# A streaming encoder step: the mixer's input projection in half-sized products, x kept in DRAM, and one pool for the mixer and the first feed-forward stage

## The chip, the cores and the metric

The kernel runs on one core of a Trainium2 chip. The metric is the time of one execution on the device in microseconds (us): the median over several runs, beside one execution that the hardware profiler recorded and from which the profile is made.

## The reference

Two layers over 1024 prompt frames and 32 frames of a running stream, of 1024 features each, in float32. Layer 0 is what matters here:

```python
def _mixer_a(h, ctx, w_in, conv_w, w_out):
    gb, gc, u = jnp.split(h @ w_in, 3, axis=-1)
    z, new_ctx = _causal_dwconv(gc * u, ctx, conv_w)      # three taps along time
    return (gb * z) @ w_out, new_ctx

def _conv_ffn(h, ctx, w_up, conv_w, w_down):
    up = h @ w_up
    upc, new_ctx = _causal_dwconv(up, ctx, conv_w)
    g, v = jnp.split(upc, 2, axis=-1)
    return (jax.nn.silu(g) * v) @ w_down, new_ctx

# layer 0
x = x + _mixer_a(_rmsnorm(x, a_norm), ...)        # w_in: 1024 x 3072, w_out: 1024 x 1024
x = x + _conv_ffn(_rmsnorm(x, ffn_norm), ...)     # w_up: 1024 x 5632, w_down: 2816 x 1024
# layer 1: attention over keys and values of x, then a second _conv_ffn; last a norm
```

## The kernel before, in words

Features lie on the 128 partitions, the 1056 frames (1024 + 32) in the free dimension, so x is 8 tiles of 128 x 1056. Each float32 product is made of three reduced-precision ones: both operands are split into a high part (a copy by ScalarE, ACT) and a low part (a subtraction by VectorE, DVE), and TensorE (PE) adds high x high, high x low and low x high (`chain`, L253, for whole products; `product`, L882, for half-sized ones). A weight of 128 output features is called a unit: 8 blocks of 128 x 128.

**Mixer, plain products.** `opening` (L712) loads x and the first three units (gc, u and gb of tile 0), splits x times the norm's gain into 16 resident tiles `xs`, and runs 3 x 72 matmuls of 352 columns: 8 blocks, 3 parts, 3 column pieces `CH`. Beside them it sums the squares of x for the norm, and near its end PE makes three products of a diagonal with ones (the "broadcasts") that spread the frames' scale `rstd` over the partitions; DVE then multiplies the results by it. `mixer` (L832) runs `make` for each of the 8 feature tiles: three units of 72 matmuls of 352 columns (`unit`, L275), u x gc, the convolution (`conv`, L520: ACT the first tap, DVE two), times gb, split into a high and a low act. After four tiles, `down` adds the first half of the output projection to x in SBUF, in pieces of 352 columns (L559 to L567). The second half goes through `tokenwise` (L435): four pieces of 264 frames (`ENDS`), after each of which the next norm of those frames is made, and x is written to DRAM (`xd`). `resident` (L504) holds its four units.

**Feed-forward, half-sized products.** `begin` (L590) and `plain` (L939) make the first four units with blocks of x split into quadrants (feature half 1 or 2, frame half 1 or 2; `part`, L480: b11, b12, b21, b22). Then DVE forms sums and differences of quadrants, again split (t1 to t4), and every `pair` (L892) makes two units by seven products of half size where a plain 2 x 2 x 2 blocking has eight: weight sums on GpSimd (POOL), 7 weight splits (`operand`, L874), 7 x 24 matmuls of 264 columns, and adds from PSUM on ACT and DVE (`late`, L959, the last frames in three pieces). Down products of two acts at a time (`stream`, L1063) are dealt out between a pair's steps; PE's result goes by ACT to a tile `xs`, and a DMA of POOL's queue adds it to x in DRAM. At the end `load` (L162) brings x back.

**What sets the order.** Each engine works through its own queue in order, and so do the DMA queues of SP and POOL. In `strict` parts the order is the program's; elsewhere a scheduler sets it. A tile comes from a rotating pool and waits until the last reader of its buffer is done: `keep` (24 of 128 x 1056 for x and its splits), `slot` (20 in the mixer, 14 in the feed-forward stages), weights `w` (4), one raw weight `wraw`. PSUM is 3 + 2 x 2 + 1 banks in the mixer, 2 + 3 x 2 in the feed-forward stages (`UPBANKS`). The mixer and the first feed-forward stage are two phases with pools of their own (L1587 to L1600).

Of the kernel before, what the change touches and what calls it, by code (L numbers as in the profile page):

```python
# [26 lines left out]
TT = SEQ + DEC  # L27
# [17 lines left out]
SLOTS = 20  # L45
# [41 lines left out]
class Net:  # L87
# [134 lines left out]
    def weights(self, src, gain=None, keep=False, cuts=((0, 8),), raw=None):  # L222
        nc = self.nc
        raw = raw or self.wp.tile([128, NK, 128], F32, name="wraw", bufs=1)
# [8 lines left out]
        h, l = (self.keep(n, [128, NK, 128], F32R) if keep else self.wp.tile([128, NK, 128], F32R, name=n, tag="w")  # L233
# [19 lines left out]
    def chain(self, ps, w, xs, c, ks=None):  # L253
# [3 lines left out]
        for i in ks or range(n):  # L257
            (xh, xl), (wh, wl) = xs[i], w[i]
            nc.tensor.matmul(ps, wh, xh[:, c[0]:c[1]], start=(i == 0), stop=False)  # L259
            nc.tensor.matmul(ps, wh, xl[:, c[0]:c[1]], start=False, stop=False)  # L260
            nc.tensor.matmul(ps, wl, xh[:, c[0]:c[1]], start=False, stop=(i == n - 1))  # L261
# [173 lines left out]
    def tokenwise(self, weight, acts, x, scale, units):  # L435
# [14 lines left out]
        for c in ENDS:  # L450
            cs, n = slice(*c), c[1] - c[0]
            if c is ENDS[-1]:
# [85 lines left out]
    def down_steps(self, units, acts, x, done=None, lag=False):  # L538
# [3 lines left out]
        banks = self.singles() if lag else iter(self.dbank, None)  # L542
# [47 lines left out]
    def begin(self, x, early, late):  # L590

# [3 lines left out]
        us = [self.slot("u", [128, WID]) for _ in range(2)]  # L595
        one, two = (slice(*c) for c in HALVES)
        orders = tuple(range(NK)), LATER
# [18 lines left out]
        def second(k):  # L616
            q = x[k + k2]
            self.nc.vector.tensor_sub(q[:, two], q[:, two], x[k][:, one])
            self.nc.vector.tensor_sub(q[:, one], q[:, two], q[:, one])

        for i in range(2):
# [30 lines left out]
        sums = [(n, k, x[k + d][:, h]) for n, ks, d, h in (  # L652
            ("t1", range(k2), 0, one), ("t3", (2, 3), 0, two), ("t2", range(k2), k2, two), ("t3", (0, 1), 0, two),
            ("t4", range(k2), k2, one)) for k in ks]
        for k in range(k2):
            self.job(lambda k=k: first(k), 1.4)
        for k in range(k2):
            self.job(lambda k=k: second(k), 1.4)
        todo = [made(*t) for t in sums]
        for (high, _), (_, low) in zip(todo + [(None, None)], [(None, None)] + todo):  # L660
            if high:
                self.job(high, 0)
            if low:
                self.job(low, 0.7)
# [47 lines left out]
    def opening(self, x, gain):  # L712
# [35 lines left out]
        def evict(u, i):  # L748
            for p, d in spread(CH[i], before[u]):
# [11 lines left out]
        before = (0, PAD, 0)  # L761
        out = [self.slot("gc"), self.slot("u", [128, TC + PAD]), self.slot("gb")]
        banks = [[self.dbank()[:, :c[1] - c[0]] for c in CH] for _ in range(2)]
# [20 lines left out]
        sq = [self.slot("sq") for _ in range(NK)]  # L784
        for m in range(NK):
            ACT.activation(sq[m], x[m], AF.Square)
            if m:
                DVE.tensor_add(sq[0], sq[0], sq[m])
# [7 lines left out]
        banks.append([self.dbank()[:, :c[1] - c[0]] for c in CH])  # L796
# [4 lines left out]
        ps = self.bank("s")[:SIDE, :n]  # L801
        for i in range(n):
            PE.matmul(ps[:, i:i + 1], sq[0][:, i * SIDE:(i + 1) * SIDE], self.ones[:, :1], start=True, stop=True)
# [10 lines left out]
        self.chain(banks[2][1], ws, xs, CH[1])  # L814
        for i, c in enumerate(CH):
# [4 lines left out]
            ps = self.bank("sos"[i])[:, :c[1] - c[0]]  # L820
            PE.matmul(ps, self.ones[:SIDE], dg[:, b].rearrange("p n c -> p (n c)"), start=True, stop=True)
            ACT.activation(self.rs[:, slice(*c)], ps, AF.Copy)
        for i, c in enumerate(CH):
            if i == 2:
                self.chain(banks[2][i], ws, xs, c)
            for u in range(2):
                for p, d in spread(c, before[u]):
                    DVE.tensor_mul(out[u][:, d], out[u][:, d], self.rs[:, p])
            DVE.tensor_mul(out[2][:, slice(*c)], banks[2][i], self.rs[:, slice(*c)])
        return xs, out  # L830

    def mixer(self, x, xs, opened, after):  # L832
        a, nc = self.a, self.nc
# [869 lines left out]
```

## Time and profile before

| | us |
|---|---|
| median of 3 runs (2506.28 to 2509.9) | 2508.73 |
| the profiled execution | 2509.51 |
| its span, first to last instruction | 2507.7 |
| PE busy | 2460.4 (98%) |
| DVE busy | 1521.1 (61%) |
| ACT busy | 1216.9 (49%) |
| POOL busy | 890.3 (36%) |
| PE's granted clock, mean | 0.995 |

Matmuls are pipelined, so one's duration is longer than the distance from one to the next; the distance is read from the number of matmuls in a stretch in which PE never waits. Instructions of `strict` parts carry the line of a helper (L73 before, L72 after), others their own. A wait is put down to the instruction that released it last.

### The profile page before, as it was taken

How to read it: one execution, taken by the hardware profiler on the slowest of the kernel's cores; microseconds unless marked ns; L12 is line 12 of the kernel's file. 1: busy time of each engine (PE TensorE's matmuls, PEld its weight loads, DVE VectorE, ACT ScalarE, POOL GpSimd, SP SyncE). 2: the span in 40 equal slices, each digit the busy share in tenths (PEclk: the TensorE clock that was granted, in tenths of full speed). 3: DMA queues.
4: the chain of work that ended last, by engine and by line, in shares of the span. 5: the costliest groups of instructions: out<-in, count | busy, mean ns of one | idle time of the engine just before them, and what ended most of it. 6: DMA issues, size and time to landing. Idle time of an engine off the chain costs nothing. (4 is left out here: it accounts for less than half of the span.)

```text
span 2507.7 us, 47246 instructions
## 1 busy us (share of the span) xinstructions
PE 2460.4 (98%) x18484; PEld 2424.6 (97%) x18484; DVE 1521.1 (61%) x2622; ACT 1216.9 (49%) x2394; POOL 890.3 (36%) x969
## 2 busy tenths in 40 slices
PE   8999999999999999999999999999999999999997
PEld 8999999999999999998999999999999999999997
DVE  6434448755555555666677667665874555555566
ACT  4111124645555555445666666643554555555554
POOL 0000012444443344452544445412244444433442
PEclk9999999999999999999999999999999999999998
DMA  3111222476666666532322233373247766666662
GB/s 121 46 48 43 60 88 82 88 121 118 121 119 113 120 112 121 134 114 66 83 71 77 75 80 81 78 250 100 70 93 124 119 119 116 114 117 120 120 153 70
DMA packets 145583, 254.76 MB, mean 102 GB/s; under 512 B 22352, under 2 KB 58320, under 8 KB 145360
## 3 DMA queue, kind: packets, MB, share of 16 engines
q0 software_dynamic: 44032, 86.53, 24.3%
q1 hardware_dynamic: 101328, 165.21, 22.1%
q8 instruction: 145, 2.38, 0.4%
q14 instruction: 78, 0.64, 0.1%
HBM read 130.52 MB, written 113.04 MB: 97 GB/s over the span
## 5 line engine op out<-in xcount | busy, mean ns | idle before, releaser
L889 PE MATMUL pb_p<-b,wb 128*128 128x264 f32 x6720 | 895.2, 285 | 1.9 <-ACT u L931 1.9
L889 PEld LDWEIGHTS pb_p<-b,wb 128*128 128x128 f32 x6720 | 850.3, 188 | 2.3 <-ACT u L931 2.3
L1078 POOL DMA_DIRECT2D xd<-xs x288 | 261.9, 914 | 495.0 <-ACT xs L1076 486.7
L1076 ACT ACTIVATE xs<-pb_d 128x264 f32<-128x264 f32 x576 | 218.4, 387 | 349.2 <-PE pb_d L261 310.3
L259 PE MATMUL pb_d<-acth,wb 128*128 128x264 f32 x1152 | 327.9, 285 | 1.5 <-ACT xs L1076 1.5
L260 PE MATMUL pb_d<-actl,wb 128*128 128x264 f32 x1152 | 327.4, 284 | 0.0
L261 PE MATMUL pb_d<-acth,wb 128*128 128x264 f32 x1152 | 327.2, 285 | 0.0
L259 PE MATMUL pb_d<-xh,wh 128*128 128x384 f32 (+2 forms) x816 | 269.1, 330 | 0.9 <-DVE x L564 0.7
L261 PE MATMUL pb_d<-xh,wl 128*128 128x384 f32 (+2 forms) x816 | 266.4, 326 | 0.0
L260 PE MATMUL pb_d<-xl,wh 128*128 128x384 f32 (+2 forms) x816 | 266.2, 326 | 0.0
L532 DVE SCALAR_TENSOR_TENSOR y<-u,cv,y 128x1058 f32<-128x1058 f32 x178 | 228.8, 1329 | 52.1 <-ACT y L528 52.0
L259 PEld LDWEIGHTS pb_d<-acth,wb 128*128 128x128 f32 x1152 | 216.7, 188 | 2.4 <-ACT xs L1076 2.1
L260 PEld LDWEIGHTS pb_d<-actl,wb 128*128 128x128 f32 x1152 | 216.9, 188 | 0.0
L261 PEld LDWEIGHTS pb_d<-acth,wb 128*128 128x128 f32 x1152 | 216.9, 188 | 0.0
L514 POOL COPY u<-cv 128x4 f32<-128x4 f32 x96 | 65.1, 678 | 374.5 <-DVE u L845 274.5
L236 ACT ACTIVATE wh<-wraw 128x1024 fp32r<-128x1024 f32 x63 | 66.8, 1061 | 247.9 <-PE pb_o L260 114.9
L879 DVE TENSOR_TENSOR wb<-wr,wb 128x512 fp32r<-128x512 f32 x196 | 153.0, 782 | 54.8 <-ACT wb L878 44.5
L879 DVE TENSOR_TENSOR wb<-ws,wb 128x512 fp32r<-128x512 f32 x160 | 121.2, 759 | 98.8 <-ACT wb L878 98.8
L911 POOL TENSOR_TENSOR ws<-wr 128x512 f32<-128x512 f32 x80 | 123.4, 1543 | 135.4 <-DMA wr<-in_w_up 108.3
L259 PEld LDWEIGHTS pb_d<-xh,wh 128*128 128x128 f32 x816 | 154.1, 189 | 1.8 <-issue 1.0
L878 ACT ACTIVATE wb<-wr 128x512 fp32r<-128x512 f32 x196 | 123.4, 629 | 66.4 <-PE pb_p L889 58.2
L260 PEld LDWEIGHTS pb_d<-xl,wh 128*128 128x128 f32 x816 | 154.3, 189 | 0.3
(383 smaller groups left out, 5063.6 us busy)
## 6 DMA issues: line engine op xcount, KB each, us to landing
xd<-xs POOLq DMA_DIRECT2D x288, 264.0 KB, 4.3
wr<-in_w_up SPq DMA_DIRECT2D x168, 256.0 KB
wr<-in_w_down SPq DMA_DIRECT2D x80, 256.0 KB
wraw<-in_w_in SPq DMA_DIRECT2D x21, 512.0 KB
xd<-x SPq DMA_DIRECT2D x64, 132.0 KB
x<-xd POOLq DMA_DIRECT2D x32, 264.0 KB, 5.3
wraw<-in_w_kq SPq DMA_DIRECT2D x16, 512.0 KB
xd<-x SPq DMA_DIRECT2D x16, 264.0 KB
```

What stands on the lines that cost most here:

```text
L236: nc.scalar.activation(h[:, i:j], raw[:, i:j], AF.Copy)
L259: nc.tensor.matmul(ps, wh, xh[:, c[0]:c[1]], start=(i == 0), stop=False)
L260: nc.tensor.matmul(ps, wh, xl[:, c[0]:c[1]], start=False, stop=False)
L261: nc.tensor.matmul(ps, wl, xh[:, c[0]:c[1]], start=False, stop=(i == n - 1))
L514: self.nc.gpsimd.tensor_copy(v, st.rearrange("p (a b) -> p a b", b=2))
L532: self.nc.vector.scalar_tensor_tensor(y, u[:, i:i + TC], w[:, i:i + 1], y, op0=OP.mult, op1=OP.add)
L878: nc.scalar.activation(t[:, 0], src, AF.Copy)
L879: nc.vector.tensor_sub(t[:, 1], src, t[:, 0].bitcast(F32))
L889: nc.tensor.matmul(ps[:, q, :QB], w[:, i, k], t[:, j, cs], start=(begin and k == 0 and n == 0), stop=(end and k == len(b) - 1 and n == 2), ...
L911: getattr(self.nc.gpsimd, "tensor_" + op)(dst, x, y)
L1076: nc.scalar.activation(t[:, q * QB:(q + 1) * QB], ps, AF.Copy)
L1078: nc.gpsimd.dma_start(d, t, accum_op=OP.add)
```

## The change

The mixer now runs in the feed-forward's pool (14 slots, `UPBANKS`), in one phase with the first feed-forward stage.

- `opening` gets its third gate's last chain ahead of the broadcasts, and loads one unit more.
- Tile 1's three units are made by plain products of 352 columns, from the `xs` tiles. Meanwhile DVE norms the 8 tiles of x in place, and as PE lets `xs` tiles go, ACT and DVE split x into quadrants (`part`) and form the sums t1 to t4 (`sums`, taken out of `begin`).
- gc and u of tile 2 go through `plain`: half-sized blocks, no product saved.
- The other 16 units are 8 pairs: (gc, u) of tiles 3 to 7, and gb of tiles 2 and 3, 4 and 5, 6 and 7. What follows of a unit (u x gc, taps, gate, split) is dealt out two steps behind each product (`put_off`).
- x as loaded is spilled to DRAM at the start. The first four acts of the output projection go through `stream` in twos, which adds to it there, in pieces of 264 columns; then x is loaded back by POOL's queue, and `tokenwise` does the last four acts, with the first two acts' products of six tiles ahead (`ahead=2`).

```diff
     def tokenwise(self, weight, acts, x, scale, units, ahead=0):
...
+            early = [next(banks)[:, :n] for _ in range(6)] if ahead and c is ENDS[0] else []
+            for m, ps in enumerate(early):
+                self.chain(ps, weight(m), acts, c, range(ahead))
             for m in range(NK):
-                ps = next(banks)[:, :n]
-                self.chain(ps, weight(m), acts, c)
+                ps = early[m] if m < len(early) else next(banks)[:, :n]
+                self.chain(ps, weight(m), acts, c, range(ahead, g) if m < len(early) else None)
...
     def opening(self, x, gain, after):
...
+        h, l = self.weights(a["w_in"][after])
...
         self.chain(banks[2][1], ws, xs, CH[1])
+        self.chain(banks[2][2], ws, xs, CH[2])
         for i, c in enumerate(CH):
...
         for i, c in enumerate(CH):
-            if i == 2:
-                self.chain(banks[2][i], ws, xs, c)
...
+    def mixer(self, x, after):
+        with self.strict():
+            xs, opened, w = self.opening(x, 0, NK + 1)
+        for m in range(NK):
+            self.spill(x, m)
...
+        with self.strict():
+            two = [weight(2 * NK + 1)]
+            for i, c in enumerate(CH):
+                self.chain(banks[0][i], w, xs, c)
+                if i:
+                    scaled(0, i - 1)
+                if i < 2:
+                    for m in LATER[2 * i:2 * i + 2]:
+                        norm(m)
+            two.append(weight(1, self.slot))
+            scaled(0, 2)
+            for m in LATER[4:]:
+                norm(m)
...
+            for n in range(NK + 1):
+                for u, k in ((0, LATER[n:n + 1]), (1, LATER[n - 1:n] if n else ())):
+                    for t, c in zip(banks[u + 1], CH):
+                        self.chain(t, two[u], xs, c, k)
+                if n:
+                    parts(LATER[n - 1])
+                if n in (3, 5):
+                    sums[n // 2 - 1]()
+                    sums[n // 2 + 3]()
...
+        put_off = gate(0, opened[2]) + parts[0] + gate(1, one[2]) + parts[1]
+        for i, (t, gates) in enumerate(((3, 0), (2, 1), (4, 0), (5, 0), (4, 1), (6, 0), (7, 0), (6, 1))):
+            if i in (1, 3):
+                for _ in fill:
+                    pass
+                fill, n, at, span = self.stream(a["w_out"][i - 1:i + 1], acts[i - 1:i + 1]), many, 0, 7 * (i // 2 + 2)
+            steps = self.pair(a["w_in"][top], a["w_in"][low], b, us)
+            for todo in steps if i else [steps[j] for j in (0, 2, 1, 3, 4, 5, 6)]:
+                for f in todo + tuple(put_off[:2]):
+                    f()
...
+        for m in range(NK):
+            self.load(x, m, nc.gpsimd)
+        ws = self.resident(a["w_out"][4:], True)
+        with self.strict():
+            self.tokenwise(ws, acts[4:], x, after, self.first(0), 2)
...
-    with net.phase(SLOTS):
+    with net.phase(UPSLOTS, banks=UPBANKS):
         net.fresh = 0
-        with net.strict():
-            opened = net.opening(x, 0)
-        net.mixer(x, *opened, net.normalise(x, 1))
-    with net.phase(UPSLOTS, banks=UPBANKS):
+        net.mixer(x, net.normalise(x, 1))
...
-        "w_out": down_units(i["w_a_out"][0]),
+        "w_out": down_units(i["w_a_out"][0], (2, 2, 4)),
```

Three places show how the queues change. The first is PE's queue at the end of the opening: `pb_...` are PSUM tiles, `xh`, `xl`, `wh`, `wl` the high and low parts of x and a weight, `dg,ones` the broadcasts. Before:

```order
L73 MATMUL pb_d<-xh,wl 128x352
L73 MATMUL pb_s<-dg,ones 128x352
L73 MATMUL pb_o<-dg,ones 128x352
L73 MATMUL pb_s<-dg,ones 128x352
L73 MATMUL pb_d<-xh,wh 128x352
```

Now, at the same place:

```order
L72 MATMUL pb_p<-xh,wh 128x352
L72 MATMUL pb_p<-xl,wh 128x352
L72 MATMUL pb_p<-xh,wl 128x352
L72 MATMUL pb_d<-dg,ones 128x352 x3
L72 MATMUL pb_p<-xh,wh 128x352
```

The last chain of 24 matmuls moved from behind the broadcasts to ahead of them; what follows them now is the next unit.

The second is DVE's queue, where it multiplies the opened units by `rstd`. `gc`, `u`, `gb` are units, `y` the convolved one, `actl` an act's low part. Before:

```order
L73 TENSOR_TENSOR gc<-gc,rstd 128x352
L73 TENSOR_TENSOR u<-u,rstd 128x320
L73 TENSOR_TENSOR u<-u,rstd 128x32
L845 TENSOR_TENSOR u<-u,gc 128x1024
L845 TENSOR_TENSOR u<-u,gc 128x32
L73 TENSOR_TENSOR gb<-pb_d,rstd 128x352
L532 SCALAR_TENSOR_TENSOR y<-u,cv,y 128x1058 x2
L853 TENSOR_TENSOR y<-y,gb 128x1024
```

Now, with `x_99` to `x_106` the eight tiles of x, `wl` a weight's low part and `wraw` the weight as loaded:

```order
L72 TENSOR_TENSOR gb<-pb_p,rstd 128x320
L72 TENSOR_TENSOR gb<-pb_p,rstd 128x32
L72 TENSOR_TENSOR wl<-wraw,wh 128x1024
L72 SCALAR_TENSOR_TENSOR x_99<-x_99,gain,rstd 128x1056
L72 SCALAR_TENSOR_TENSOR x_103<-x_103,gain,rstd 128x1056
L864 TENSOR_TENSOR u<-u,gc 128x1024
L864 TENSOR_TENSOR u<-u,gc 128x32
L72 TENSOR_TENSOR u<-pb_p,rstd 128x352
L72 SCALAR_TENSOR_TENSOR x_100<-x_100,gain,rstd 128x1056
L72 SCALAR_TENSOR_TENSOR x_104<-x_104,gain,rstd 128x1056
L72 TENSOR_TENSOR u<-pb_p,rstd 128x352
```

The convolution of tile 0 moved far back; a weight's low part and the norms of x stand in its place, with the next unit's scalings between them.

The third is the DMA queue of SP. Before, weights of the input projection follow the loads of the opening:

```order
L724 DMA x_106<-in_x 128x1056
L727 DMA wr<-in_w_in 128x1024
L708 DMA cv<-in_st_a 128x32
L709 DMA cv<-in_cw_a 128x24
L227 DMA wraw<-in_w_in 128x1024 x21
```

Now one weight follows, then 16 spills of x (`xd_...`) with five half blocks of `plain` and the first pair among them; their last rows, and the next weights:

```order
L159 DMA xd_81<-x_105 128x528
L159 DMA xd_82<-x_105 128x528
L986 DMA wr<-in_w_in 128x512
L159 DMA xd_83<-x_106 128x528
L159 DMA xd_84<-x_106 128x528
L986 DMA wr<-in_w_in 128x512 x2
L227 DMA wraw<-in_w_in 128x1024 x2
```

The second weight, of tile 1's u, moved behind all the spills.

More of the change, by code (lines that the diff above doesn't have):

```diff
@@ L44 @@
 LATER = tuple(k + i for k in range(NK // 2) for i in (0, NK // 2))
-SLOTS = 20
 UPSLOTS = 14
@@ L433, in ending, with tokenwise @@
             scaled(y, m, c, None if m > 5 else r)
-    def tokenwise(self, weight, acts, x, scale, units):
+    def tokenwise(self, weight, acts, x, scale, units, ahead=0):
         g = len(acts)
@@ L588, in late_square, with sums @@
         return c[1] < TT
-    def begin(self, x, early, late):
+    def sums(self, x, order=range(5)):
         k2, b = NK // 2, self.b
-        us = [self.slot("u", [128, WID]) for _ in range(2)]
         one, two = (slice(*c) for c in HALVES)
-        orders = tuple(range(NK)), LATER
         def made(n, k, src):
@@ L619, in second, with begin @@
             self.nc.vector.tensor_sub(q[:, one], q[:, two], q[:, one])
+        blocks = (("t1", range(k2), 0, one), ("t3", (2, 3), 0, two), ("t2", range(k2), k2, two), ("t3", (0, 1), 0, two),
+                  ("t4", range(k2), k2, one))
+        sums = [(n, k, x[k + d][:, h]) for n, ks, d, h in (blocks[i] for i in order) for k in ks]
+        jobs = [(lambda k=k, f=f: f(k), 1.4) for f in (first, second) for k in range(k2)]
+        todo = [made(*t) for t in sums]
+        for (high, _), (_, low) in zip(todo + [(None, None)], [(None, None)] + todo):
+            if high:
+                jobs.append((high, 0))
+            if low:
+                jobs.append((low, 0.7))
+        return jobs
+    def begin(self, x, early, late):
+        k2, b = NK // 2, self.b
+        us = [self.slot("u", [128, WID]) for _ in range(2)]
+        orders = tuple(range(NK)), LATER
         for i in range(2):
@@ L651, in begin @@
         self.ready = []
[L652 to L664, printed above, removed]
+        for f, cost in self.sums(x):
+            self.job(f, cost)
         self.job(lambda: None, 0, label="sums")
@@ L710, in convs, with opening @@
         return st, cw, out
-    def opening(self, x, gain):
+    def opening(self, x, gain, after):
         nc, a = self.nc, self.a
@@ new lines, in weight, with scaled, norm, parts @@
+        def weight(i, keep=None):
+            h, l = self.weights(a["w_in"][i], keep=keep)
+            return [(h[:, k], l[:, k]) for k in range(NK)]
+        def scaled(u, i):
+            self.normalised(one[u], banks[u][i], CH[i])
+        def norm(m):
+            self.nc.vector.scalar_tensor_tensor(x[m], x[m], self.gain[:, 0, m:m + 1], self.rs, op0=OP.mult, op1=OP.mult)
+        def parts(m):
+            for i in range(2):
+                for f in self.part(x, i, m):
+                    f()
```

166 lines of the change are left out of this document (107 added, 59 removed).

## The prediction

> **What bounds the kernel now.** First the page: the span, and how busy each engine is.
>
> ```profile
> span 2507.7 us, 47246 instructions
> PE 2460.4 (98%) x18484; PEld 2424.6 (97%) x18484; DVE 1521.1 (61%) x2622; ACT 1216.9 (49%) x2394; POOL 890.3 (36%) x969
> ```
>
> TensorE (PE) has work in 98% of the span. Of the 47 us without, the stage table below shows where the ones near this change lie. Its columns: stretch in us, its length, then busy time and (in brackets) instructions of PE, PE weight load, VectorE (DVE), ScalarE (ACT), GpSimd (POOL), then granted clock, DMA share and GB/s.
>
> ```profile
> 0.00:25.00 25.00, 17.84 (x79) 15.45 (x80) 14.87 (x18) 16.94 (x20) 0.70 (x6) 1.00 0.71 260
> 200.00:250.00 50.00, 50.00 (x314) 50.00 (x313) 19.89 (x30) 7.67 (x8) 2.08 (x3) 1.00 0.14 43
> 350.00:400.00 50.00, 48.35 (x397) 47.76 (x396) 34.59 (x84) 18.96 (x45) 16.42 (x20) 1.00 0.39 125
> 400.00:450.00 50.00, 49.89 (x409) 49.68 (x409) 47.01 (x68) 29.52 (x58) 16.18 (x14) 1.00 0.12 38
> 450.00:500.00 50.00, 48.27 (x391) 47.58 (x390) 37.36 (x52) 27.44 (x49) 21.38 (x24) 1.00 0.49 99
> 550.00:600.00 50.00, 50.00 (x413) 50.00 (x411) 24.59 (x39) 24.33 (x47) 24.27 (x29) 1.00 0.71 124
> 1750.00:1800.00 50.00, 48.19 (x394) 47.54 (x393) 41.75 (x83) 22.80 (x51) 11.79 (x16) 1.00 0.26 86
> 1800.00:1850.00 50.00, 49.16 (x402) 48.95 (x401) 48.86 (x61) 31.84 (x54) 19.86 (x15) 1.00 0.15 49
> 1850.00:1900.00 50.00, 49.11 (x401) 48.77 (x400) 27.61 (x39) 25.74 (x55) 21.87 (x27) 1.00 0.71 120
> ```
>
> 200 to 250 us lies in the mixer: PE is busy throughout, 314 matmuls, all 352 columns wide, so one takes 50/314 = 159.2 ns. 550 to 600 us lies in the first feed-forward stage, where half-sized products of 264 columns run without a gap: 50/413 = 121.1 ns. Between the two, 88 columns cost 38.1 ns, or 0.433 ns each; 6.8 ns are left that do not depend on width. The clock is 1.00 in both. So in the mixer time is PE's columns, and what another engine does there costs nothing until PE has to wait for it. DVE is at 19.89 of 50 us and POOL at 2.08: there is room for the added work, on the average.
>
> The other rows show what a joint costs, where a stage of plain products goes over into half-sized ones: 400 to 450 us falls 4 matmuls short of 413 and 450 to 500 us 22 short, that is 0.5 and 2.7 us; in the second feed-forward stage the three stretches from 1750 to 1900 us miss 19 + 11 + 12 = 42, or 5.1 us. DVE is busy 47.01 and 48.86 of 50 us just there. The waits of PE name what came late:
>
> ```profile
> PE pb_p L73 <- DVE x L73: 3.3, 2, 1.7
> PE pb_p L889 <- ACT u L931: 1.9, 2, 1.1
> PE pb_d L259 <- ACT xs L1076: 1.5, 2, 0.9
> ```
>
> **The change part by part.** The forecast is made on the profiled execution: 2509.51 us, 1.8 more than its span; the median of the runs shown is 2508.73, 0.8 below it.
>
> *Fewer columns: -19.7 us.* Sixteen of the 24 input units become eight pairs. A unit was 8 x 3 x 3 = 72 matmuls of 352 columns, so 1152 go; a pair is 7 products of 24 matmuls of 264, so 1344 come. Two more units go from 144 wide to 192 narrow ones (no product saved), and the first half of the output projection from 288 to 384. Together 1584 x 159.2 = 252.2 us leave and 1920 x 121.1 = 232.5 us come. All lie on the path, since PE is the path. The output projection's second half stays as it is, 384 matmuls of 264.
>
> By the sustained roofline in the Trainium skill's "TensorE: Matmul & The Clock Gate", section "Back-to-back issue gap" (81 ns a matmul at 128 columns, 131 at 512), a matmul costs about 64 ns before its first column; an estimate from it is 99 ns for 264 columns and 110 for 352, and the sum would be 189.5 - 174.5, a loss of 15.0 us. By that rule the change is bad. The two rows above speak against it: 121.1 and 159.2 ns leave only 6.8 ns a matmul.
>
> *The opening.* The third gate's last chain now stands ahead of the three broadcasts of the row scale, not behind them.
>
> ```profile
> 45.24 0.76 PE L73 MATMUL pb_s<-dg,ones 88*128 88x352 f32 x2
> ...
> 46.42 0.76 PE L73 MATMUL pb_s<-dg,ones 88*128 88x352 f32 x2
> ```
>
> ```profile
> 46.52 0.52 DVE L73 TENSOR_TENSOR gc<-gc,rstd 128x352 f32<-128x352 f32 x1 [2.36 <-ACT rstd L73]
> 46.97 0.52 DVE L73 TENSOR_TENSOR u<-u,rstd 128x352 f32<-128x352 f32 x1
> ```
>
> That moves the broadcasts by 24 x 159.2 ns = 3.8 us: DVE gets the scale at 46.52 + 3.8 = 50.3 us, PE is through at 46.42 + 0.6 + 3.8 = 50.8. Nothing is lost there: PE runs the chain it would have run later. But all that DVE does with the scale starts 3.8 us later, and now there is more of it. The prices (the number ahead of the bar is busy time, then the mean ns):
>
> ```profile
> L237 DVE TENSOR_TENSOR wl<-wraw,wh 128x1024 fp32r<-128x1024 f32 x27 | 33.0, 1222 | 7.3 <-ACT wh L236 7.3
> ...
> L73 DVE TENSOR_TENSOR b<-x,b 128x528 fp32r<-128x528 f32 x32 | 22.6, 749 | 0.9 <-ACT b L73 0.7
> ...
> L845 DVE TENSOR_TENSOR u<-u,gc 128x1024 f32<-128x1024 f32 x8 | 9.8, 1226 | 0.0
> ...
> L73 DVE SCALAR_TENSOR_TENSOR xl<-x,gain,xh 128x1056 fp32r<-128x1056 f32 x7 | 9.1, 1317 | 1.9 <-ACT xh L73 1.8
> ...
> L73 DVE TENSOR_TENSOR x<-x,x 128x528 f32<-128x528 f32 x8 | 7.7, 979 | 0.1
> ...
> L73 DVE TENSOR_TENSOR x<-x 128x528 f32<-128x528 f32 x8 | 6.6, 826 | 0.1
> ...
> L73 DVE TENSOR_TENSOR wb<-wr,wb 128x512 fp32r<-128x512 f32 x2 | 1.3, 690 | 1.8 <-ACT wb L73 1.8
> ...
> L962 DVE TENSOR_TENSOR u<-mid,pb_p 128x264 f32<-128x264 f32 x5 | 2.1, 426 | 8.3 <-PE pb_p L889 8.3
> ...
> L962 DVE TENSOR_TENSOR u<-mid,pb_p 128x232 f32<-128x232 f32 x5 | 1.9, 389 | 0.0
> ...
> L962 DVE TENSOR_TENSOR u<-mid,pb_p 128x32 f32<-128x32 f32 x5 | 0.9, 179 | 0.0
> ```
>
> DVE starts successive 352-column scalings 0.45 us apart. Until the second scaled third of the next unit it has 9 of these and 3 short ones (4.3), a weight's low half (1.2), four norms of x (x gain and scale, as the 1317 ns row: 5.2), one u x gc (1.23 + 0.18 for its last 32 columns) and two scalings (0.9): 13.0, done at 63.3. PE has 72 matmuls from 50.8 (62.3) and 6 more (63.2) before it needs the PSUM bank which that scaling frees. So the wait is 0.1; with every duration in full it is 1.5. I take **0.7**.
>
> *The joint.* DVE goes on: another weight (1.2), the last third (0.6), four norms (5.2), then 8 blocks of x split twice (16 x 0.71 = 22.6/32 a piece: 11.3), 8 half sums ((7.7 + 6.6)/16 = 0.89 each: 7.2) and two weight blocks (1.4): 26.9 us, done at 90.2, and 88.8 for the last but one block. PE comes to that block's product after 216 - 78 more wide matmuls from 63.3 (85.3) and 9 narrow ones: 86.4. A wait of 2.4 us; none, if DVE issues these as closely as the scalings (0.85 of their durations); 6, at full durations without overlap. The measured joint of the first feed-forward stage, 2.7 us, lies between: I take **2.7**. Behind it, the remaining products of x give PE 23 us, in which DVE has 16 more splits and 8 sums; the seven products of the first pair follow.
>
> *The first output products.* In the same stretch DVE carries the first pair, two conv's and two gates:
>
> ```profile
> L532 DVE SCALAR_TENSOR_TENSOR y<-u,cv,y 128x1058 f32<-128x1058 f32 x38 | 50.4, 1346 | 14.7 <-ACT y L528 14.6
> ...
> L879 DVE TENSOR_TENSOR wb<-wr,wb 128x512 fp32r<-128x512 f32 x26 | 21.0, 815 | 7.8 <-PE pb_d L261 4.9 <-ACT wb L878 2.8
> ...
> L930 DVE TENSOR_TENSOR mid<-mid,pb_p 128x528 f32<-128x528 f32 x5 | 3.5, 693 | 0.0
> ...
> L246 DVE TENSOR_TENSOR actl<-y,acth 128x1024 fp32r<-128x1024 f32 x8 | 9.7, 1218 | 1.0 <-ACT acth L245 1.0
> ```
>
> From the second product of that pair to the low half of the second gated unit stand 7 weight splits (5.7), 4 splits of x (2.8), 3 taps (4.0), a u x gc (1.4), two gate products (2.8), two low halves (2.8) and 9 PSUM adds (0.69 x 3 + 2 x (0.43 + 0.39 + 0.18) = 4.1): 23.6 us. PE has eight products there, 8 x 24 x 121.1 ns = 23.3 us, and then the first output chain waits for that low half with all later products queued behind it. Even on paper; between 0 and 2.4 us; I take **1.2**.
>
> *The pairs.* Without output products beside it a pair is 7 x 2.9 = 20.3 us of PE; DVE has 7 splits, 9 adds, a scaling and two taps for it: 5.7 + 4.1 + 1.4 + 2.7 = 13.9 us. PE hides them, as the 550 us row does. Nothing.
>
> *The end.* x now waits in DRAM, so 16 loads on the POOL queue bring it back, and the last four units' weights are split late.
>
> ```profile
> DMA packets 145583, 254.76 MB, mean 102 GB/s; under 512 B 22352, under 2 KB 58320, under 8 KB 145360
> ...
> x<-xd POOLq DMA_DIRECT2D x32, 264.0 KB, 5.3
> ...
> L1078 POOL DMA_DIRECT2D xd<-xs x288 | 261.9, 914 | 495.0 <-ACT xs L1076 486.7
> ```
>
> Issue is 16 x 0.91 = 14.6 us and landing 5.3. Tiles come free as the last pair's first two products end, 14 us before its last; and PE has the early chains, 36 + 36 narrow matmuls = 8.7 us, before it needs the first sum with x. So hidden; if all loads began only with the last product, the last would land at 19.9 us, where the chains reach its bank at about 18.4: 1.5 us at worst. The second weight's low half, though, stands on DVE behind the last three adds into u (1.0): 1.0 + 1.2 + about 0.2 = 2.4 us after the last product, and PE wants it after 14 matmuls, 1.7 us: **0.7**, between 0 and 1.5.
>
> *The loads and spills at the start.* 16 spills of 264 KB and 5 blocks of 256 KB (5.5 MB) stand on SP's queue ahead of the next unit's weight. At the 260 GB/s of the first 25 us they take 21 us and the weight is there at about 49 us; DVE's turn for it is at 54.6. Hidden by 5 us. If that cover is gone, every us is PE's, since the norms stand behind this weight on DVE.
>
> Sum: 2509.5 - 19.7 + 0.7 + 2.7 + 1.2 + 0.7 = 2495.1; against the median 0.8 less, **2494.3 us**. With all joints at zero it is 2489.0; with all at their upper ends (1.5 + 6 + 2.4 + 1.5 + 1.5 = 12.9) 2501.9.
>
> **The rivals.** *The joints eat most of it.* DVE is the bound from 50 to 135 us and each wait comes at its upper end, with one or two that I do not see (a slot of the shared pool, now 14 instead of 20, that comes free late; GpSimd's sums behind a halo copy). For it: 48.86 of 50 us DVE busy in the other joint. Against it: that joint cost 5.1 us, not 12.9. Time 2501.9 to 2508, on either side of "same".
>
> *The spills hold the weight up: slower.* If SP's 5.5 MB move slower than about 122 GB/s, the weight comes over 19 us after DVE's turn and the time passes 2513.7. At 102 GB/s, the mean of the whole kernel, they end at 25 + 54 = 79 us, 82 with landing and cast: 27 us late, 2494.3 + 27 = 2521. For it: in the second feed-forward's dense stretches 120 to 124 GB/s took 0.71 of the DMA engines. Against it: 260 GB/s at the same share in the first stretch, with plain loads, and 125 GB/s at a share of 0.39 where plain x rows were written.
>
> *Matmuls priced by the piece: slower.* If width did not matter, 336 more matmuls would cost 336 x 121.1 ns = 40.7 us: 2508.7 + 40.7 + 5 = 2554. Only the skill's line above speaks for some of it (with its estimate, 2529); the rows do not.
>
> *No product saved.* If the pairs were only rearranged, the columns would be equal; but 7 x 24 matmuls for 8 x 24 is counted in the instructions. No chance given.
>
> **How the numbers follow.** The forecast (2489 to 2501.9) 0.77. Joints at their worst 0.14, of it 0.06 below 2503.7. Spills 0.04, pieces 0.02, other slower mishaps 0.01; a gain beyond 2489 (the feed-forward's first blocks are fetched earlier) 0.02. A measurement of this kernel can tell 0.2%, 5 us, from no change. So faster (below 2503.7) 0.85, same 0.08, slower (above 2513.7) 0.07. The range 2489 to 2504 leaves out 0.02 below and 0.15 above.
>
> **What would show it.** Right: the mixer's narrow matmuls 121 ns apart, and tokenwise beginning some 14 us earlier; PE waits of 1 to 3 us in all for x's splits near 86 us, one near 133 for the low half of a gated unit, one just behind the last pair for a weight's low half. Wrong: a PE wait over 5 us between 60 and 135 us, a weight that lands after 55 us, PE waits for xs or for reloaded x, narrow matmuls over 125 ns, or the feed-forward's own joint grown.

## The result, and the profile after

The changed kernel takes 2490.04 us, median of 6 runs (2488.15 to 2492.84), the kernel before 2508.93 (6 runs beside them, 2506.28 to 2510.4): a ratio of 0.9926, 95% interval 0.9916 to 0.9936. The forecast was 2494.3, so the gain is 18.9 us where 14.4 were expected. The profiled execution took 2491.21 us with this page:

```profile
span 2489.2 us, 48534 instructions
PE 2441.0 (98%) x18820; PEld 2404.4 (97%) x18820; DVE 1586.6 (64%) x2720; ACT 1285.5 (52%) x2565; POOL 979.3 (39%) x1049
```

PE has 336 matmuls more, as counted, and 19.4 us less busy time; DVE 65.5 us more. The stage table, with the columns of before:

```profile
25.00:50.00 25.00, 25.00 (x167) 24.77 (x167) 11.93 (x16) 9.76 (x16) 0.00 (x0) 1.00 0.48 172
50.00:75.00 25.00, 25.00 (x153) 24.28 (x152) 24.44 (x37) 8.01 (x13) 0.31 (x2) 1.00 0.14 43
75.00:100.00 25.00, 25.00 (x185) 25.00 (x184) 24.79 (x40) 10.96 (x24) 5.37 (x5) 1.00 0.16 53
...
200.00:250.00 50.00, 50.00 (x413) 50.00 (x413) 25.19 (x39) 18.34 (x39) 19.54 (x20) 1.00 0.56 103
250.00:300.00 50.00, 50.00 (x413) 50.00 (x413) 27.10 (x45) 19.36 (x38) 17.30 (x16) 1.00 0.45 90
300.00:350.00 50.00, 48.04 (x382) 47.76 (x382) 32.42 (x66) 17.68 (x34) 17.96 (x30) 0.97 0.55 189
350.00:400.00 50.00, 49.62 (x404) 48.81 (x403) 40.85 (x90) 23.22 (x53) 11.29 (x17) 1.00 0.20 68
```

At 200 us PE now does 413 narrow matmuls in 50 us (121.1 ns each by this count) where 314 wide ones stood. From 50 to 100 us DVE is busy 49.2 of 50 us, and PE still never stops. The loss stands elsewhere: from 300 to 350 us PE misses 31 matmuls and its granted clock is 0.97. PE's waits up to 520 us:

```profile
PE pb_p L72 <- ACT xh L72: 6.4, 2, 5.5
PE pb_p L72 <- DVE wl L237: 2.0, 1, 2.0
PE pb_p L1004 <- ACT u L1046: 1.1, 1, 1.1
PE pb_d L259 <- ACT xs L1195: 0.9, 2, 0.6
PE pb_p L72 <- DVE xl L72: 0.7, 1, 0.7
PE pb_d L72 <- DVE acc L72: 0.2, 1, 0.2
```

The first row and the fifth are the first loads, as in before. Between 12 and 323 us there is no wait at all. New is the one of 2.0 us for a weight's low half (`wl`), and the wait of 1.65 us for x at the feed-forward's start is gone.

Spans by stage, from the start times of matmuls in the timeline (first matmul of the output projection's second half, of the first feed-forward stage, of attention, of the second feed-forward stage; last matmul; end):

| us | to output projection | output projection | feed-forward 1 | attention | feed-forward 2 | tail | span |
|---|---|---|---|---|---|---|---|
| before | 339.77 | 51.62 | 722.34 | 654.03 | 730.72 | 9.23 | 2507.7 |
| before, profiled again | 339.90 | 51.62 | 722.87 | 656.22 | 730.29 | 9.24 | 2510.1 |
| after | 319.71 | 53.39 | 724.14 | 654.62 | 730.08 | 7.29 | 2489.2 |
| e1_resident_first | 319.26 | 55.17 | 724.81 | 651.91 | 730.34 | 7.30 | 2488.8 |
| e2_two_phases | 319.52 | 52.08 | 722.27 | 649.85 | 729.91 | 6.85 | 2480.5 |
| e3_no_ahead | 319.79 | 50.26 | 723.98 | 650.85 | 728.33 | 7.28 | 2480.5 |
| e4_dve_5 | 326.17 | 53.64 | 724.35 | 654.80 | 729.95 | 7.30 | 2496.2 |
| e5_late_halves | 320.36 | 53.78 | 724.14 | 655.86 | 729.66 | 6.88 | 2490.7 |
| e6_two_phases_no_ahead | 319.53 | 51.45 | 722.03 | 655.93 | 730.45 | 6.85 | 2486.2 |
| e7_dve_2 | 322.71 | 52.39 | 722.99 | 651.18 | 729.48 | 7.30 | 2486.0 |
| e8_spill_twice | 319.89 | 53.60 | 724.08 | 654.26 | 730.20 | 7.55 | 2489.6 |
| e9_broadcasts_first | 320.38 | 53.63 | 723.90 | 656.50 | 728.15 | 7.29 | 2489.9 |
| e10_halves_behind | 318.70 | 50.27 | 722.38 | 654.88 | 729.57 | 7.48 | 2483.3 |
| e11_halves_two_phases | 320.22 | 52.05 | 721.97 | 651.63 | 730.52 | 7.10 | 2483.5 |

So of the 18.5 us between the spans, 20.1 come in the mixer's products; 1.8 are given back in the output projection, 1.8 in the first feed-forward stage, 0.6 in attention; 0.6 and 1.9 come from the second feed-forward stage and the tail.

The first column also holds a difference that is no work of the kernel: in every profile the first wide matmuls start 0.293 us apart in place of 0.160, half clock by their distance, and the granted clock turns full at some time between 14.65 us (e10) and 18.26 us (e7). Each us later costs 0.45 us. In before that was at 16.09 us, in after at 16.75, so 0.3 us of the first column is the clock's.

### The profile page after: what moved, and what is told of

Its sections match the earlier page's. It is cut to its first block, busy times and chain, and to the rows that moved or that the text cites. A ratio compares the mean times of both kernels' runs of the same rounds, so it can differ in the third digit from the quotient of the medians.

```text
span 2489.2 us, 48534 instructions
## 1 busy us (share of the span) xinstructions
PE 2441.0 (98%) x18820; PEld 2404.4 (97%) x18820; DVE 1586.6 (64%) x2720; ACT 1285.5 (52%) x2565; POOL 979.3 (39%) x1049
## 5 line engine op out<-in xcount | busy, mean ns | idle before, releaser
L1004 PE MATMUL pb_p<-b,wb 128*128 128x264 f32 x8208 | 1082.7, 284 | 2.1 <-ACT u L1046 2.1
L1004 PEld LDWEIGHTS pb_p<-b,wb 128*128 128x128 f32 x8208 | 1033.6, 188 | 2.5 <-ACT u L1046 2.5
L259 PE MATMUL pb_d<-acth,wb 128*128 128x264 f32 x1280 | 364.2, 285 | 2.7 <-ACT xs L1195 2.7
L261 PE MATMUL pb_d<-acth,wb 128*128 128x264 f32 x1280 | 363.6, 285 | 0.0
L259 PEld LDWEIGHTS pb_d<-acth,wb 128*128 128x128 f32 x1280 | 240.8, 188 | 3.8 <-ACT xs L1195 3.6
L261 PEld LDWEIGHTS pb_d<-acth,wb 128*128 128x128 f32 x1280 | 241.2, 189 | 0.0
L259 PE MATMUL pb_d<-xh,wh 128*128 128x384 f32 (+1 forms) x576 | 190.6, 331 | 0.9 <-DVE x L567 0.7
L261 PE MATMUL pb_d<-xh,wl 128*128 128x384 f32 (+1 forms) x576 | 188.6, 327 | 0.0
L260 PE MATMUL pb_d<-xl,wh 128*128 128x384 f32 (+1 forms) x576 | 188.4, 327 | 0.0
L993 ACT ACTIVATE wb<-ws 128x512 fp32r<-128x512 f32 x192 | 120.5, 628 | 98.2 <-PE pb_p L1004 90.0
L1460 ACT ACTIVATE pt<-pb_d 128x512 fp32r<-128x512 f32 (+1 forms) x160 | 85.3, 551 | 108.6 <-PE pb_d L1457 104.3
L1461 DVE TENSOR_TENSOR pt<-pb_d,pt 128x512 fp32r<-128x512 f32 (+1 forms) x160 | 98.1, 631 | 57.6 <-ACT pt L1460 57.4
```

Source lines behind the costliest of these rows:

```text
L993: nc.scalar.activation(t[:, 0], src, AF.Copy)
L1004: nc.tensor.matmul((ps[q] if type(ps) is list else ps[:, q])[:, :QB], w[:, i, k], t[:, j, cs], start=(begin and k == 0 and n == 0), stop=( ...
L1460: nc.scalar.activation(pt[:, :n], ps[:, :n], AF.Copy)
L1461: nc.vector.tensor_sub(pt[:, 512:512 + n], ps[:, :n], pt[:, :n].bitcast(F32))
```

## The experiments

My theory after the result: the gain is PE's columns, and DVE only just covers the joints; the give-back is the reload of x. The rivals: the joints have plenty of room; the give-back is the order on DVE, as forecast; the shared pool made part of the gain.

**How thin is the cover: DVE later by a known amount.** In `mixer`, behind the first extra weight, with n = 5 and n = 2:

```diff
             two = [weight(2 * NK + 1)]
+            d = streams[0]
+            for _ in range(n):
+                nc.vector.tensor_mul(one[0][:, d], opened[0][:, d], opened[1][:, d])
```

> The changed kernel with five more DVE products of 128 x 1024 behind the first extra weight's low half, in a tile that is overwritten later: 5 x 1.13 = 5.7 us of work just ahead of the joint, whose results nobody reads. Theory A (DVE only just keeps up: the splits of x end at 86.2 us where PE starts the half-sized product at 85.9 and needs the last of them about 1 us later, and the third bank is free some 0.5 us ahead of its need): PE stands still for 4.5 to 5.5 us in one place between 60 and 70 us, once, since PE is then as late as DVE; with a stretch at half clock behind it 1.7 more: 2495 to 2497 us. Theory B (the joints cost nothing because there is room): under 1 us, 2490 to 2491 us.

> As the run with five extra DVE products, with two. Five delayed the bank by 5.1 us and PE by 3.9; so two should delay it by 2.05 us, of which the cover at the bank (0.87 us by the trace: free at 62.86, needed at 63.73) takes the most part of one: PE stands still for 1.0 to 1.3 us near 65 us. Theory A (PE's clock halves for 3.4 us where PE was idle for more than half of the 3.4 us before): 1.2 of 3.4 us is too little, no half clock follows, and the output projection starts 1.0 to 1.4 us later than in the changed kernel (319.7), at 320.7 to 321.1. Theory B (any wait of over 1 us costs a stretch at half clock): 1.7 more, 322.4 to 322.8.

PE's timeline with five, then with two (start, duration, and in brackets the idle time before it):

```profile
68.03 0.66 PE L72 MATMUL pb_p<-xh,wh 128*128 128x352 f32 x1 [3.94 <-DVE u L72]
```

```profile
65.94 0.43 PE L72 MATMUL pb_p<-xh,wh 128*128 128x352 f32 x1 [1.30 <-DVE u L72]
```

Theory A holds, a little under its numbers with five: the waits are 3.94 and 1.30 us, at the one bank, and a room for five products did not exist. With five, the output projection starts 6.5 us late: 3.9 of wait, about 1.5 of half clock, the rest in slow starts behind the waits, in 0.2 us before 40 us and in a small wait near 147 us; median 2494.06 us (4 runs). With two there is no half clock behind the wait and the output projection starts at 322.71 where A said 320.7 to 321.1 (one run, 2488.25 us): 0.7 of the difference were there at 18 us already, since the clock turned full 1.5 us later than in the changed kernel, the rest of the joint's is the slow start behind the wait, and 0.5 came near 143 us:

```profile
143.09 0.39 PE L259 MATMUL pb_d<-acth,wb 128*128 128x264 f32 x1 [0.23 <-ACT xs L1198]
```

This is not the forecast's wait for the low half of a gated unit, which was ready at 134.81 us, ahead of its use. An output product waited for ACT's copy of an earlier one; the copy stood behind a tap of a convolution, and that tap behind GpSimd's halo copy (the few earlier frames that a convolution needs in front of its first). The scheduler had put the product u x gc that the halo copy follows at 139.59 us, in the changed kernel at 133.90, so the run does not measure how much room the low half has.

**The broadcasts' place undone.** The chain `banks[2][2]` goes back behind the loop of the broadcasts.

> The changed kernel with the opening's order of before: the third gate's last chain behind the three broadcasts. DVE gets the scale 3.8 us earlier, at 46.7 us, and is done with the last split of x at about 82.4 in place of 86.2. Theory A (the cover of DVE's work is thin, but it is there: 0.87 us at the bank, 0.2 us at the last split): PE does the same work without a wait either way, and the output projection starts at 319.1 to 320.3 us (319.7, and the spread of the first loads). Theory B (the broadcasts' move cost PE the forecast's 0.7 us or more in short gaps that no record shows): it starts at 318.5 to 319.0.

The output projection starts at 320.38 us (one run, 2491.87 us): no loss and no gain beyond the clock's start, which was at 18.01 us here and at 16.75 in the changed kernel and accounts for 0.6 of the 0.7 us between them. But my picture was wrong. DVE's timeline:

```profile
59.66 0.53 DVE L72 TENSOR_TENSOR u<-pb_p,rstd 128x352 f32<-128x352 f32 x1 [3.45 <-PE pb_p L72]
...
69.54 0.70 DVE L72 TENSOR_TENSOR b<-x,b 128x528 fp32r<-128x528 f32 x1
```

DVE starts 3.3 us earlier, then stands 3.45 us for PE's next product, which is not earlier; it begins the splits of x at 69.54 us, in the changed kernel at 69.31. The later scale costs nothing because DVE would have waited that time anyway (its first product with the scale starts at 47.16 us here, at 50.49 in the changed kernel).

**Twice the spills.** `for m in range(2 * NK): self.spill(x, m % NK)`.

> The changed kernel with every spill of x done twice: 16 more DMAs of 264 KB, 4.3 MB, on SP's queue ahead of the next unit's weight. By the forecast's rate (260 GB/s) the queue is through at about 66 us instead of 49, and the weight 11 us after DVE's turn for it at 54.6: PE would lose about 10 us and the half clock behind it, and the output projection start at about 331 us. By the rate of the changed kernel's own trace (353 to 389 GB/s from 20 to 35 us, the spills done at 35), 4.3 MB take 12 us more: done at 47, the weight there at about 50, ACT's turn for it is at 51.8: nothing lost, start at 319.5 to 320.5 us.

The second: 319.89 us (one run, 2491.69 us). The DMA engines are full for some 12 us longer, as these windows show, from the changed kernel and then from this one; yet ACT casts the weight at 51.94 us where it did at 51.77, and PE waits for nothing from there to the output projection.

```profile
30.00:35.00 5.00, 5.00 (x33) 5.00 (x32) 4.79 (x5) 3.64 (x5) 0.00 (x0) 1.00 0.98 353
```

```profile
40.00:45.00 5.00, 5.00 (x44) 5.00 (x43) 2.19 (x8) 1.03 (x4) 0.00 (x0) 1.00 1.06 387
45.00:50.00 5.00, 5.00 (x32) 4.79 (x31) 0.00 (x0) 0.00 (x0) 0.00 (x0) 1.00 0.43 162
```

**The wait behind the last pair.** Four edits. The resident units asked for first (`ws = self.resident(...)` ahead of the loop of `self.load`):

> The changed kernel with one thing moved: the four resident units of the output projection's second half are asked for ahead of the sixteen loads that bring x back. Theory A (the reload crowds out the second unit's weight, which landed about 10 us after its issue, and ACT's cast of it held up a gated unit's split behind it): the 2.0 us wait of PE behind the last pair goes, and with it the 3.4 us at half clock that follow; 2490.0 - 2.0 - 1.7 = 2486.3 us. Theory B (the forecast's: the low half stands on DVE behind the last three adds into u, whenever its weight lands): a wait of 0.7 to 2.0 us stays, and the time lies at 2488.5 to 2490. Theory C: x now comes back too late and DVE's first adds wait for it; slower, 2491 to 2495.

None of the three came out whole: 2490.73 us (4 runs), and the wait, 3.2 us in all, is now in three pieces. SP's order did not change (it waits for slots), the loads of x moved behind, and ACT waits for the third unit:

```profile
324.00 1.06 ACT L236 ACTIVATE wh<-wraw 128x1024 fp32r<-128x1024 f32 x1 [4.11 <-DMA wraw<-in_w_out]
```

By the times it is the reload again, delaying a later weight: this unit was issued at 315.60 us, and the DMA engines' share is 1.00 and 1.03 from 310 to 320 us. No run changes that alone. Without early chains (`tokenwise(...)` without its last argument, 2):

> The changed kernel without the early chains: the second half of the output projection goes tile by tile from the start, all four acts each. Theory A (the forecast's: the early chains hide the last gated units' splits and the reload of x, 8.7 us of PE): PE waits 4 to 9 us more, 2494 to 2499 us. Theory B (the last acts' first halves are ready 1.9 us after the last product by the trace, at 321.6 us, and the second unit's weight is needed later than in the changed kernel): PE waits about 1.2 us for an act, none for the weight, and no stretch at half clock follows; 2487 to 2490 us.

Theory B, for the output projection: no wait for the weight, no half clock, 50.26 us; the wait for an act is 0.35 us where B said 1.2. The weight is cast no sooner (at 319.03 us); the early chains, which the forecast counted as cover, bring PE to it before it is ready. The time is 2483.82 us (4 runs), under B's 2487 to 2490, with attention at 650.85 us.

The second halves of x later, first on POOL's queue, then on SP's (`hold`, read where a unit is loaded, makes the units' own loads keep the program's order there too; those lines are left out here):

```diff
         for m in range(NK):
-            self.load(x, m, nc.gpsimd)
+            x[m] = self.keep(f"x{m}")
+            (d, cs), late = self.spilled(m)
+            nc.gpsimd.dma_start(x[m][:, cs], d)
+            self.at(3 + m, lambda m=m, d=late[0], cs=late[1]: nc.gpsimd.dma_start(x[m][:, cs], d))
```

```diff
-            self.at(3 + m, lambda m=m, d=late[0], cs=late[1]: nc.gpsimd.dma_start(x[m][:, cs], d))
+            self.at(3 + m, lambda m=m, d=late[0], cs=late[1]: self.tc.keep_in_program_order(nc.sync.dma_start(x[m][:, cs], d)))
+        self.hold = True
         ws = self.resident(a["w_out"][4:], True)
+        self.hold = False
```

> The changed kernel with the reload of x in two parts: the first 528 frames of each tile as before, the second 528 only while the output projection's first piece runs (they are first added to 23 us later). Theory A (from 305 to 320 us the DMA engines are full with 4.2 MB of x, and the second resident weight, issued at 309.35, lands only at about 319): 2.1 MB are gone from there, the weight lands by about 315, ACT's cast and DVE's queue behind it move up, the wait of 1.96 us shrinks to 0.5 or less, and no stretch at half clock follows. The output projection with its norms (53.4 us from its first matmul to the feed-forward's first) shortens to 50 to 51.5 us. Theory B (the weight's low half stands behind the adds into u on DVE, whenever it lands): the wait stays at 1 us or more, and the stage at 52.5 us or more. Time: 2486 to 2488 us by A, if the attention stage stays as it is; 2489 to 2490 by B.

> The changed kernel with the second 528 frames of x brought back by SP's queue, behind the four resident units and each behind a first write of the output projection's first piece, so that they cannot run ahead as they did in the last try. Theory A (4.2 MB of reload fill the DMA engines from 305 to 320 us and delay the second resident unit from its issue at 309.4 to about 319): it lands by 315, its cast follows a gated unit's at 316.6, its low half is ready about 322.0 on DVE behind the adds into u, PE wants it at 321.4: a wait of 0.3 to 0.7 us in place of 1.96, under half of a stretch of 3.4 us, so no half clock; 50.2 to 52.1 us from the output projection's first matmul to the feed-forward's first, in place of 53.4. Theory B (the order on DVE alone makes the wait): 1.5 us or more stays and the stage takes 53 us or more. Time by A 2486 to 2488 us with the attention stage as in the changed kernel, by B 2490.

The first is no test: nothing on POOL's queue stood between the halves, so it ran ahead, issued the last of the sixteen loads at 314.28 us, and the wait was 2.34 us (2489.38 us, 5 runs). The second is theory A: a wait of 0.35 us, no half clock and 50.27 us for the stage; 2485.06 us (4 runs), ratio to before 0.9905, interval 0.989 to 0.992. The DMA windows of the changed kernel and of this one, from 305 us:

```profile
305.00:310.00 5.00, 5.00 (x44) 5.00 (x43) 4.26 (x6) 1.91 (x4) 4.30 (x9) 1.00 0.97 313
310.00:315.00 5.00, 5.00 (x44) 5.00 (x43) 2.68 (x7) 1.56 (x2) 2.63 (x5) 1.00 1.01 371
315.00:320.00 5.00, 5.00 (x43) 5.00 (x43) 3.72 (x6) 1.46 (x2) 0.00 (x0) 1.00 1.03 400
```

```profile
305.00:310.00 5.00, 5.00 (x43) 5.00 (x42) 3.65 (x5) 1.78 (x3) 1.59 (x3) 1.00 0.95 304
310.00:315.00 5.00, 5.00 (x43) 5.00 (x43) 3.28 (x7) 1.06 (x1) 0.00 (x0) 1.00 0.64 234
315.00:320.00 5.00, 5.00 (x43) 5.00 (x42) 4.62 (x12) 3.43 (x6) 0.00 (x0) 1.00 0.62 213
```

With half the reload the DMA engines are no longer full, and the unit is there before ACT turns to it.

**One pool or two.** The first feed-forward stage in a phase of its own, alone, without early chains, and with the reload in two parts:

```diff
         net.mixer(x, net.normalise(x, 1))
+    with net.phase(UPSLOTS, banks=UPBANKS):
         f, acc, parts = net.normed(x, "x", None)
```

> The changed kernel with the pool shared no longer: a phase of its own for the first feed-forward stage, with the same 14 slots and the same PSUM banks. Theory A (the gain is the columns alone, and the wait of 1.65 us for a norm of x that the kernel before had at the start of the feed-forward went because of the mixer's PSUM banks and order): 2490 us, within 1. Theory B (the shared pool took that wait away, since the first feed-forward weights are fetched while the mixer still runs): the wait is back and the first weight blocks land later; 2491.7 to 2494.

> Both edits that were faster, together: phases of their own and no early chains. If each takes away the same thing (the wait for the second weight and the half clock behind it), nothing adds up: 2483 to 2485 us, with the output projection's stage at 50 to 52 us. If they are independent, twice the gain: 2477 to 2479 us. By their stages I expect the first: 50.3 us for the output projection, 722.3 for the feed-forward.

> The same reload in two parts, and the first feed-forward stage in a phase of its own, so that its weight blocks do not stand ahead of the resident units on SP's queue. If the reload is what delays the unit, nothing more is gained in the output projection: 50.2 to 52.1 us there. The feed-forward stage takes 722.0 to 722.4 us, as in both runs with phases of their own, if its 1.8 us over that in the changed kernel come from where its last waits fall; 724 if they come from the reload. The whole, with an attention stage between 650 and 656 us: 2482 to 2488 us.

PE's waits from 300 to 380 us with two phases and the reload in two parts, then with one pool and the same reload:

```profile
PE pb_p L72 <- DVE x L72: 1.6, 1, 1.6
PE pb_p L72 <- DVE wl L240: 0.4, 1, 0.4
```

```profile
PE pb_p L72 <- DVE wl L240: 0.4, 1, 0.4
PE pb_d L72 <- DVE acc L72: 0.2, 1, 0.2
```

The wait of 1.65 us at the feed-forward's start is there in all profiles with two phases (both of before, e2, e6, e11) and in none with one: DVE's order is the same, but the new phase's first PSUM tile waits until DVE has added the old phase's last one to x: in e11 that add ends at 372.13 us and PE starts at 372.27; in e10 PE starts at 368.97, ahead of the same add's end at 370.63. So one pool is worth 1.2 us (e3 against e6) to 1.8 us (e10 against e11) in the output projection's stage. It also has a cost: alone, two phases take 0.35 us of wait in place of 1.96, since five feed-forward blocks and two small loads no longer stand ahead of the resident unit on SP's queue (issue at 307.16 in place of 309.35 us). The whole was 2484.13, 2488.06 and 2486.0 us (4 runs each). Theory B of e2 had the returning wait, but not the sign. In e6 the two gains did not add up, since both take away the same wait for the unit, and attention took 655.93 us where e2's took 649.85. The test that e11 was to make of the first feed-forward stage fell through: that stage is short in e10 too, with one pool (see the last section).

**The spread of one kernel.**

> The kernel before, profiled a second time, for the spread of one kernel's stages. If stages differ between executions only by the first loads and by where the 3.4 us stretches fall that set the clock, then up to the output projection's second half it takes 339.8 us within 0.7, from there to the feed-forward's first product 51.6 within 0.2 with the 1.65 us wait at its end, and the feed-forward stage 722.3 or, with one more stretch at half clock near its end, 724.0; the attention stage 654 within 3. The tail behind the last matmul, 9.2 us in the first profile and 6.8 to 7.5 in all profiles with the change, tells whether the change shortened it (9.2 again) or not (about 7).

One run, 2511.91 us. The first two stages repeat within 0.13 us, the third within 0.5; attention took 656.2. The tail is 9.24 us again, so the change did shorten it, by about 1.9 us; what in the closing instructions does it I did not trace.

## Why the prediction was right, and what its steps missed

**Fewer columns, -19.7.** Right. The output projection's second half starts 20.06 us earlier, with no wait on the way. The two prices were a little low, since a window's count takes in the matmuls that its ends cut: from start to start they are 160.4 ns (before, 50 to 330 us) and 121.7 (after, 140 to 319 us). With these the step gives -20.4, and the clock's later start in the changed kernel takes 0.3 of it back.

By an estimate from the sustained roofline of the Trainium skill's "TensorE: Matmul & The Clock Gate", section "Back-to-back issue gap", the change would have lost 15.0 us. The trace disagrees, with some 122 ns for 264 columns and 160 for 352.

**The opening, +0.7: nothing; the joint, +2.7: nothing; the first output products, +1.2: nothing.** The mechanism was right and the sizes too large; the lower ends held, of which the joint's was given: "none, if DVE issues these as closely as the scalings". The changed kernel's DVE:

```profile
62.33 0.52 DVE L72 TENSOR_TENSOR u<-pb_p,rstd 128x352 f32<-128x352 f32 x1
...
64.39 5.00 DVE L72 SCALAR_TENSOR_TENSOR x<-x,gain,rstd 128x1056 f32<-128x1056 f32 x4
...
82.39 3.79 DVE L72 TENSOR_TENSOR b<-x,b 128x528 fp32r<-128x528 f32 x6
```

The bank is free at 62.85 (forecast 63.3); PE needs it at 63.73, by the row below (forecast 63.2). The splits start 0.62 us apart, forecast 0.71, and are done at 86.2, forecast 90.2; the first narrow product starts at 85.9 us and takes the last blocks later. The gated unit's low half is ready at 133.97; PE takes it at 136.24, behind 13 matmuls of the pair that the scheduler put in between.

```profile
63.73 0.32 PE L72 MATMUL pb_p<-xh,wh 128*128 128x352 f32 x1
```

```profile
136.24 0.28 PE L260 MATMUL pb_d<-actl,wb 128*128 128x264 f32 x1
```

I added durations where start to start counts. The cover left, the time by which something is ready ahead of its need, is 0.9 us at the bank, and e4 and e7 show that no more is there. At the splits it is at least 0.7 us: in e7 they end 1.0 us behind the first narrow product's start (89.24 against 88.22), in the changed kernel 0.3, and PE waits in neither. What the opening's step had wrong besides is that the broadcasts' later place would count: e9.

**The pairs, 0.** Right: 413 matmuls in each 50 us from 200 to 300.

**The end, +0.7 and the reload hidden.** The step that failed is "so hidden". PE never waited for x; but sixteen loads filled the DMA engines from 305 to 320 us, and the second resident unit, issued behind feed-forward blocks at 309.35, was there at 319.16. On ACT its cast stood ahead of a gated unit's, on DVE that unit's low half and the adds stood ahead of the weight's. SP's, ACT's, DVE's and PE's timelines:

```profile
309.35 0.66 SPq L227 DMA_DIRECT2D wr<-in_w_out  x1
```

```profile
319.16 1.06 ACT L236 ACTIVATE wh<-wr 128x1024 fp32r<-128x1024 f32 x1 [1.89 <-DMA wr<-in_w_out]
```

```profile
320.37 0.19 DVE L883 TENSOR_TENSOR actl<-y,acth 128x32 fp32r<-128x32 f32 x1 [1.35 <-ACT acth L882]
...
322.27 1.22 DVE L237 TENSOR_TENSOR wl<-wr,wh 128x1024 fp32r<-128x1024 f32 x1
```

```profile
323.54 0.39 PE L72 MATMUL pb_p<-acth,wl 128*128 128x264 f32 x1 [1.96 <-DVE wl L237]
```

That makes 1.96 us, and about 1.5 for the half clock behind it (below), where 0.7 was forecast. With half the reload or the blocks out of the way 0.35 remain (e10, e2): that is the forecast's own term, the low half behind the adds.

**Loads and spills at the start, 0.** Right, with more room than worked out: 353 to 389 GB/s in place of 260, and twice the spills still hide.

**Not in the forecast:** the phase boundary's 1.65 us gained; stretches at half clock, here and in the later stages; the tail.

That the time lies inside the range is partly luck. The median is 1.0 us above the range's lower end of 2489, and the 1.8 us of the first feed-forward stage, which no term of the forecast had, are more than that. Attention (+0.6), the second feed-forward stage (-0.6) and the tail (-1.9 us) were not forecast either and happen to cancel them.

The rivals: the joints did not eat the gain, but 1 to 2 us more of work for DVE would have begun to; the spills did not hold the weight up; matmuls are not priced by the piece.

The best versions here are 5 to 6 us below the changed kernel: phases of their own (2484.13 us, ratio to before 0.9899, 0.9882 to 0.9915), no early chains (2483.82, 0.9899, 0.9884 to 0.9914), the reload in two parts (2485.06). By the stage table the first owes 3.2 us of its 8.7 to the two stages that it changes and 4.8 to attention, which it does not address; the last owes 4.9 of 5.9 to the two stages. But 1.9 and 1.8 us of these are the first feed-forward stage's, where the clock's grid decides and not the edit (last section), so what the edits themselves are shown to save is their gain in the output projection: 1.3, 3.1 and 3.1 us in this order. The third's interval, 0.989 to 0.992, overlaps the changed kernel's.

## What to carry to other kernels

Where a second engine that works in order is nearly full beside the one that sets the time (DVE from 50 to 100 us here, 49.2 of 50), sum its work by the distance from start to start, and look where it waits for the bound engine: delays ahead of such a wait cost nothing. A transfer that nobody waits for can still cost what it holds up: add up the bytes of all queues in that stretch against what the DMA engines moved at their fullest. And an edit that takes a load from its place must be seen in the queue's order: two of mine did not move what they meant to.

## What the runs showed of the hardware

PE's granted clock is set in stretches of 3.41 us on a fixed grid: in the changed kernel it was half from 323.95 to 327.37, from 1057.82 to 1061.23 and from 1160.22 to 1167.05 us, and 1057.82 - 323.95 is 215 x 3.413. In every profile all such changes, the first turn to full clock among them, lie whole stretches apart; against the kernel's start the grid lies differently each time, and so that first turn falls anywhere from 14.65 to 18.26 us. Outside attention, a stretch runs at half clock when PE was idle for more than about half of the stretch before. Pairs of stretches from the changed kernel, from before, and from e7 (PE's busy time second, granted clock third from the end):

```profile
320.60:324.00 3.40, 1.44 (x12) 1.23 (x11) 3.10 (x6) 1.33 (x2) 0.00 (x0) 0.99 0.43 164
324.00:327.40 3.40, 3.40 (x18) 3.40 (x17) 2.54 (x5) 1.68 (x3) 0.00 (x0) 0.50 0.47 148
```

```profile
388.10:391.50 3.40, 1.75 (x15) 1.57 (x14) 3.14 (x6) 1.25 (x4) 1.68 (x2) 1.00 0.43 152
391.50:394.90 3.40, 3.40 (x31) 3.40 (x32) 2.48 (x5) 1.33 (x3) 0.75 (x1) 1.00 0.46 132
```

```profile
325.50:328.90 3.40, 1.71 (x14) 1.71 (x15) 3.40 (x7) 0.57 (x2) 0.00 (x0) 1.00 0.03 10
328.90:332.30 3.40, 3.40 (x31) 3.40 (x30) 2.55 (x6) 1.78 (x4) 0.00 (x0) 1.00 0.43 154
```

1.44 us busy of 3.4 were too few, 1.75 and 1.71 enough. In all 14 profiles together, outside the first 20 us, attention and the last 30 us, there are 14 stretches with 53% idle or more, and each is followed by half clock; none with 51% or less is. In attention half clock also follows stretches with less idle time (0 to 37%), which I cannot explain. A stretch at half clock costs about 1.5 us: narrow matmuls start 0.220 us apart in it where 0.122 is usual, wide ones 0.293 where 0.160 is. The 1.7 us that I reckoned with in the expectations, half a stretch, were too much. Whether a wait of 2 us brings it on depends on how the grid cuts it: e7's wait of 2.61 us did not, since the grid left 1.69 us of it in the pair's first stretch above, and the same two waits near the first feed-forward stage's end (1.4 and 0.7 us) did so in the changed kernel and not in before, where the grid's line fell between them. That is this stage's 1.8 us: it takes 723.9 to 724.8 us in the seven profiles with that stretch and 722.0 to 723.0 in the seven without. Attention's spread, 650 to 656.5 us, is mostly waits of PE (13.5 to 16.9 us) and stretches at half clock (3.4 to 13.7 us, of which about half counts); what is left is 634.6 to 636.0 us in all 14 profiles.

The Trainium skill's "TensorE: Matmul & The Clock Gate", section "What's actually happening", has the window, 3413 ns and free-running. The traces agree, by the distances and the first turns above. The Trainium skill's "TensorE: Matmul & The Clock Gate", section "HAM oscillation — how this bites in real kernels", asks for no idle gaps over about 3.4 us. That is too lenient here: a gap of 1.96 us sufficed.
